# A row-wise log-sum-exp: row sums shared among group reductions, two-operand adds and ScalarE accumulation, and the last row loaded whole

## The chip, the cores and the metric

The kernel runs on one core of one Trainium2 chip. The metric is the device time in microseconds (us), lower is better. The profile's span, from the first to the last instruction, is some 1.8 us shorter than that time. Times inside a profile are counted from the start of its span.

## The reference

```python
x: float32 [32, 512, 1024], standard normal
def reference(x):
    max_x = np.max(x, axis=-1, keepdims=True)
    return max_x.squeeze(-1) + np.log(np.sum(np.exp(x - max_x), axis=-1))
```

That is 16384 rows of 1024 numbers, 128 rows on each of the 128 partitions: 67.1 MB are read and 64 KB written.

## The kernel before

It takes no maximum. It computes log(sum(exp(x))) directly, and if any sum left the range 1e-15 to 1e15 it runs a slow second pass with the maximum. Rows pass through a ring of 48 rows in SBUF. ScalarE makes the exponentials in place; then the row sums are made in one of three ways: "R", a VectorE reduction of up to 4 rows; "T", a VectorE instruction for each row that adds its two halves and accumulates; "A", ScalarE's own accumulation in the exponential.

```python
RING = 48
loads = [(16, "R")] * 5 + [(13, "T"), (10, "T"), (7, "T"), (5, "T"), (4, "T"), (3, "T"), (2, "T")]
loads += [(1, "A")] * 3
LAST = NC - 1                       # NC = 128 rows on each partition
SPLIT = 3 * d // 4
...
for size, how in loads:
    ...
    load(p0, c0, size)
    for b in range(0, size, 4):
        s = min(4, size - b)
        v = ring[:, p0 + b : p0 + b + s, :]
        if how == "A":
            exp_sum(v, c0 + b)
            continue
        nc.scalar.activation(out=v, in_=v, func=AF.Exp)
        if how == "R":
            nc.vector.reduce_sum(out=sumexp[:, c0 + b : c0 + b + s], in_=v, axis=AX.X)
            continue
        for r in range(b, b + s):
            lo = ring[:, p0 + r, 0:H]
            nc.vector.scalar_tensor_tensor(
                out=lo, in0=lo, scalar=1.0, in1=ring[:, p0 + r, H:d],
                op0=ALU.mult, op1=ALU.add, accum_out=sumexp[:, c0 + r : c0 + r + 1])
...
load(p0, LAST, 1, 0, SPLIT)         # the last row comes as 3/4 and 1/4
load(p0, LAST, 1, SPLIT, d)
exp_sum(ring[:, p0, 0:SPLIT], LAST)
nc.scalar.activation(out=res[:, EARLY:LAST], in_=sumexp[:, EARLY:LAST], func=AF.Ln)
check(0, LAST, 0)                   # clamp, compare, count by a matmul
exp_sum(ring[:, p0, SPLIT:d], NC)
nc.scalar.activation(out=res[:, LAST:NC], in_=sumexp[:, NC : NC + 1], func=AF.Ln, bias=sumexp[:, LAST:NC])
nc.sync.dma_start(out=out_view, in_=res)
for i, c in ((1, LAST), (2, NC)):   # clamp and compare each part of the last sum
    ...
    add_to_count(i, last=i == 2)
nc.vector.tensor_copy(out=nbad, in_=count)
outside = nc.values_load(nbad[0:1, 0:1], ...)        # read by all five engines
with tc.If(outside > 0, ...):       # the slow pass; not taken with this input
    ...
```

## Time and profile before

| | before |
|---|---|
| time, median of 4 runs | 166.50 us (166.48 to 166.58) |
| span of the profile | 164.6 us |
| DMA share of the span | 95.2% |
| busy: ScalarE, VectorE | 116.4, 116.0 us |

The first lines are from the page of the kernel before. The first has busy time, share of the span and number of instructions for each engine. "DMA" and "GB/s" have 40 equal slices of the span: the busy share of the DMA engines in tenths, and the rate. The last two are DMA queues, with packets, megabytes, and their share of the time of 16 engines.

```profile
...
PE 0.6 (0%) x6; PEld 0.3 (0%) x6; DVE 116.0 (70%) x117; ACT 116.4 (71%) x48; POOL 0.2 (0%) x4
...
DMA  7989998997998999899899899999998999999940
GB/s 255 494 366 414 510 398 366 510 478 319 478 510 366 398 510 414 350 510 478 350 446 510 366 398 414 440 466 406 428 458 388 439 420 423 422 419 421 403 170 18
...
q1 hardware_dynamic: 2592, 67.18, 95.2%
q14 instruction: 2, 0.02, 0.0%
...
```

ScalarE (ACT) and VectorE (DVE) are busy for 71 and 70% of the span; the DMA engines never rest until the second slice from the end. This is a load stream with compute behind it. Queue 14: 2 packets, 0.02 MB. It carries the engines' instructions: by the packet records one of the two comes at 132.7 us, inside the stream, the other at 163.8 us, after it.

The next lines are groups of instructions from the same page: line, engine, operation, out<-in, shape, count, then busy us and mean ns, then the engine's idle time before them and what ended it.

```profile
...
L100 ACT ACTIVATE ring<-ring 128x4096 f32<-128x4096 f32 (+3 forms) x34 | 110.1, 3304 | 44.4 <-DMA ring<-in_x_dram 44.2
L102 DVE TENSOR_REDUCE sumexp<-ring 128x4 f32<-128x4096 f32 x20 | 87.0, 4412 | 33.8 <-ACT ring L100 33.8
L106 DVE SCALAR_TENSOR_TENSOR ring<-ring 128x512 f32<-128x512 f32 x44 | 27.7, 688 | 8.8 <-ACT ring L100 8.7
L86 ACT ACTIVATE ring<-ring 128x1024 f32<-128x1024 f32 (+2 forms) x5 | 4.3, 869 | 0.0
...
```

Both engines' idle time is waiting for data or for each other; neither sets the pace until the end. The end is this part of the timeline of before (start us, duration us, engine, line, operation; PE is TensorE, SPq the queue that issues DMAs):

```profile
...
157.33 0.69 DVE L106 SCALAR_TENSOR_TENSOR ring<-ring 128x512 f32<-128x512 f32 x1
...
158.63 1.04 ACT L86 ACTIVATE ring<-ring 128x1024 f32<-128x1024 f32 x1
...
159.79 0.24 ACT L119 ACTIVATE res<-sumexp 128x47 f32<-128x47 f32 x1
159.79 0.23 DVE L70 TENSOR_SCALAR clamped<-sumexp 128x127 f32<-128x127 f32 x1 [1.77 <-ACT ring L86]
159.94 0.83 ACT L86 ACTIVATE ring<-ring 128x768 f32<-128x768 f32 x1
...
160.76 0.40 ACT L86 ACTIVATE ring<-ring 128x256 f32<-128x256 f32 x1
...
161.07 0.19 ACT L86 ACTIVATION_READ_ACCUMULATOR ring<-ring 128x1 f32 x1
...
161.29 0.29 ACT L122 ACTIVATE res<-sumexp 128x1 f32<-128x1 f32 x1
...
161.34 0.15 DVE L129 TENSOR_SCALAR bad<-sumexp 128x1 f32<-128x1 f32 x1
161.53 0.16 DVE L133 TENSOR_TENSOR bad<-bad,sumexp 128x1 f32<-128x1 f32 x1
161.61 0.35 SPq L125 DMA_DIRECT2D out_dram<-res  x1
...
161.75 0.19 PE L66 MATMUL count<-ones,bad 128*1 128x1 f32 x2 [0.26 <-DVE bad L133]
161.97 0.15 DVE L137 CAST nbad<-count 1x1 int32<-1x1 f32 x1 [0.28 <-PE count L66]
```

ScalarE is late: the 3/4 row landed at 159.28 us by the semaphore records of the trace and is begun at 159.94; the 1/4 row landed at 159.60 and is begun at 160.76. Its last sum is read out at 161.25. From there one path goes through Ln and the output DMA, the other through VectorE and TensorE to the cast at 161.97, whose value all engines must read before they may end. A long row of waits and branches closes the program, up to 164.61.

### The profile page before, as it was taken

The numbers are of one execution on the slowest core, as the hardware profiler recorded it, in microseconds if no ns is written. First come the engines' busy times: TensorE is split into PE (matmuls) and PEld (weight loads), VectorE is DVE, ScalarE is ACT, GpSimd is POOL, SyncE is SP. The second block draws the span as 40 slices with busy tenths as digits, with TensorE's granted clock in tenths as the row PEclk, the third lists the DMA queues.
The fourth block names the chain that finished last, engine by engine and source line by source line (L and its number), as shares of the span: only waits on it lengthen the run. The fifth ranks groups of instructions, "written<-read, shape, count | busy, mean of one in ns | idle before, by whom it ended". The sixth has DMA issues, their size and how long they took to land.

```text
span 164.6 us, 297 instructions
## 1 busy us (share of the span) xinstructions
PE 0.6 (0%) x6; PEld 0.3 (0%) x6; DVE 116.0 (70%) x117; ACT 116.4 (71%) x48; POOL 0.2 (0%) x4
## 2 busy tenths in 40 slices
PE   0000000000000000000000000000000000000001
PEld 0000000000000000000000000000000000000000
DVE  0000004999789995999959998699998668665951
ACT  3000039990699709994299915998799999999992
POOL 0000000000000000000000000000000000000000
DMA  7989998997998999899899899999998999999940
GB/s 255 494 366 414 510 398 366 510 478 319 478 510 366 398 510 414 350 510 478 350 446 510 366 398 414 440 466 406 428 458 388 439 420 423 422 419 421 403 170 18
DMA packets 2594, 67.19 MB, mean 408 GB/s; under 512 B 288, under 2 KB 544, under 8 KB 1056
## 3 DMA queue, kind: packets, MB, share of 16 engines
q1 hardware_dynamic: 2592, 67.18, 95.2%
q14 instruction: 2, 0.02, 0.0%
HBM read 67.11 MB, written 0.07 MB: 408 GB/s over the span
## 4 chain that ended last, share of the span: by engine, by line
DMA 66%; DVE 19%; ACT 12%; issue 1%; SPq 0%; PE 0%; ACTq 0%; DVEq 0%
DMA ring<-in_x_dram 66%; DVE sumexp L102 19%; ACT ring L100 9%; ACT ring L86 2%; SPq L81 0%; DVE bad L133 0%; DVE bad L129 0%; ACT res L119 0%; PE count L66 0%; DVE nbad L137 0%; ACTq L100 0%; DVEq L129 0%; ACTq L119 0%
## 5 line engine op out<-in xcount | busy, mean ns | idle before, releaser
L100 ACT ACTIVATE ring<-ring 128x4096 f32<-128x4096 f32 (+3 forms) x34 | 110.1, 3304 | 44.4 <-DMA ring<-in_x_dram 44.2
L102 DVE TENSOR_REDUCE sumexp<-ring 128x4 f32<-128x4096 f32 x20 | 87.0, 4412 | 33.8 <-ACT ring L100 33.8
L106 DVE SCALAR_TENSOR_TENSOR ring<-ring 128x512 f32<-128x512 f32 x44 | 27.7, 688 | 8.8 <-ACT ring L100 8.7
L86 ACT ACTIVATE ring<-ring 128x1024 f32<-128x1024 f32 (+2 forms) x5 | 4.3, 869 | 0.0
L106 DVE DVE_READ_ACCUMULATOR ring<-ring 128x1 f32 x44 | 3.7, 83 | 0.0
L62 ACT ACT_TABLE_LOAD x1 | 1.3, 1283 | 0.7 <-PEq L170 0.7
L70 DVE TENSOR_SCALAR clamped<-sumexp 128x127 f32<-128x127 f32 x1 | 0.2, 226 | 1.8 <-ACT ring L86 1.8
L66 PE MATMUL count<-ones,bad 128*1 128x1 f32 x6 | 0.6, 164 | 161.4 <-DVE clamped L74 160.4
L86 ACT ACTIVATION_READ_ACCUMULATOR ring<-ring 128x1 f32 x5 | 0.9, 186 | 0.0
L129 DVE TENSOR_SCALAR bad<-sumexp 128x1 f32<-128x1 f32 x2 | 0.3, 154 | 0.6 <-ACT ring L86 0.5
L63 DVE MEMSET ones<- 128x1 f32 x1 | 0.1, 59 | 0.8 <-PEq L170 0.8
L66 PEld LDWEIGHTS count<-ones,bad 128*1 128x1 f32 x6 | 0.3, 80 | 161.6 <-DVE clamped L74 160.4
L133 DVE TENSOR_TENSOR bad<-bad,sumexp 128x1 f32<-128x1 f32 x2 | 0.3, 160 | 0.1
L137 DVE CAST nbad<-count 1x1 int32<-1x1 f32 x1 | 0.1, 147 | 0.3 <-PE count L66 0.3
L74 DVE SCALAR_TENSOR_TENSOR clamped<-clamped,sumexp 128x127 f32<-128x127 f32 x1 | 0.3, 294 | 0.0
L122 ACT ACTIVATE res<-sumexp 128x1 f32<-128x1 f32 x1 | 0.3, 294 | 0.0
L119 ACT ACTIVATE res<-sumexp 128x47 f32<-128x47 f32 x1 | 0.2, 242 | 0.0
L114 ACT ACTIVATE res<-sumexp 128x80 f32<-128x80 f32 x1 | 0.3, 253 | 0.0
L170 POOL MEMSET const-bfloat16-1.0<- 128x1 bf16 x1 | 0.1, 102 | 0.0
L170 POOL MEMSET const-uint8-127<- 128x1 uint8 x1 | 0.1, 101 | 0.0
L170 POOL MEMSET const-float32-0.0<- 128x1 f32 x1 | 0.1, 99 | 0.2 <-issue 0.2
L170 POOL MEMSET const-float32-1.0<- 128x1 f32 x1 | 0.1, 98 | 0.0
(1 smaller groups left out, 0.1 us busy)
## 6 DMA issues: line engine op xcount, KB each, us to landing
ring<-in_x_dram SPq DMA_DIRECT2D x1, 6656.0 KB, 33.3
ring<-in_x_dram SPq DMA_DIRECT2D x1, 5120.0 KB, 30.4
ring<-in_x_dram SPq DMA_DIRECT2D x1, 3584.0 KB, 28.7
ring<-in_x_dram SPq DMA_DIRECT2D x1, 2560.0 KB, 30.4
ring<-in_x_dram SPq DMA_DIRECT2D x1, 2048.0 KB, 31.0
ring<-in_x_dram SPq DMA_DIRECT2D x1, 1536.0 KB, 30.4
ring<-in_x_dram SPq DMA_DIRECT2D x3, 512.0 KB, 33.3
ring<-in_x_dram SPq DMA_DIRECT2D x1, 1024.0 KB, 32.5
```

Of the source, the lines that this page charges most:

```text
L62: nc.scalar.preload_act_table_set("natural_log_exp_and_others")
L66: nc.tensor.matmul(count, lhsT=bad[:, i : i + 1], rhs=ones, start=i == 0, stop=last)
L74: nc.vector.scalar_tensor_tensor(out=clamped[:, c0:c1], in0=clamped[:, c0:c1], scalar=0.0, in1=sumexp[:, c0:c1], op0=ALU.bypass, op1=ALU.n ...
L86: nc.scalar.activation(out=v, in_=v, func=AF.Exp, accum_out=sumexp[:, c : c + 1])
L100: nc.scalar.activation(out=v, in_=v, func=AF.Exp)
L102: nc.vector.reduce_sum(out=sumexp[:, c0 + b : c0 + b + s], in_=v, axis=AX.X)
L106: nc.vector.scalar_tensor_tensor(out=lo, in0=lo, scalar=1.0, in1=ring[:, p0 + r, H:d], op0=ALU.mult, op1=ALU.add, accum_out=sumexp[:, c0 + ...
L114: nc.scalar.activation(out=res[:, 0:EARLY], in_=sumexp[:, 0:EARLY], func=AF.Ln)
L122: nc.scalar.activation(out=res[:, LAST:NC], in_=sumexp[:, NC : NC + 1], func=AF.Ln, bias=sumexp[:, LAST:NC])
L129: nc.vector.tensor_scalar(out=bad[:, 3:4], in0=sumexp[:, c : c + 1], scalar1=LOW, scalar2=HIGH, op0=ALU.max, op1=ALU.min,)
L133: nc.vector.tensor_tensor(out=bad[:, i : i + 1], in0=bad[:, 3:4], in1=sumexp[:, c : c + 1], op=ALU.not_equal)
L170: nc = _bacc.Bacc("TRN2", target_bir_lowering=False, num_devices=1)
```

## The change

Its intent: share the row sums so that both engines finish just behind the stream with fewer instructions, and shorten what follows the last byte. The last row comes whole. Its sum is checked in two ways that need little after it: from below, by the maximum of 256 raw values (if that is at least -34, the sum is above 1e-15); from above, by a matmul that adds the last sums straight into the count. The exponential of the last row goes to PSUM, so that the raw row stays. Three engines read the flag.

```diff
-    loads = [(16, "R")] * 5 + [(13, "T"), (10, "T"), (7, "T"), (5, "T"), (4, "T"), (3, "T"), (2, "T")]
-    loads += [(1, "A")] * 3
+    loads = [
+        "R8 R8", "R8 R8", "R8 R8", "R7 R6 A A", "R6 R5 A A A", "R5 R4 A", "R5 R4", "R5 T3",
+        "R3 A A A", "R3 A", "R2 T2", "R3", "R1 A", "T2", "T1", "A", "A",
+    ]
...
+    ENGINES = [mybir.EngineType.SP, mybir.EngineType.Activation, mybir.EngineType.DVE]
... (the loop over the loads, with declarations that spare waits which an earlier wait already covers)
+                o = v if c < LAST else last_exp
+                exp = nc.scalar.activation(out=o, in_=v, func=AF.Exp, accum_out=sums)
...
-    load(p0, LAST, 1, 0, SPLIT)
-    load(p0, LAST, 1, SPLIT, d)
... (the two sums of the split row and their two checks go)
+    nc.scalar.activation(out=res[:, EARLY:NC], in_=sumexp[:, EARLY:NC], func=AF.Ln)
     nc.sync.dma_start(out=out_view, in_=res)
... (clamp and compare of rows 0 to 126, as before)
+    nc.tensor.matmul(count, lhsT=bad[:, 0:1], rhs=far, start=True, stop=False)
+    nc.vector.reduce_max(out=bad[:, 2:3], in_=last_row[:, 0, 0 : d // 4], axis=AX.X)
+    nc.vector.tensor_scalar(out=bad[:, 1:2], in0=bad[:, 2:3], scalar1=LOG_LOW, scalar2=None, op0=ALU.is_lt)
+    nc.tensor.matmul(count, lhsT=bad[:, 1:2], rhs=far, start=False, stop=False)
+    nc.tensor.matmul(count, lhsT=sumexp[:, LAST:NC], rhs=ones, start=False, stop=True)
+    nc.vector.tensor_scalar(out=fine, in0=count, scalar1=HIGH, scalar2=None, op0=ALU.is_lt)
+    all_fine = nc.values_load(fine[0:1, 0:1], engines=ENGINES, ...)
+    with tc.If(all_fine < 1, ...):
```

More of the change, by code (lines that the diff above doesn't have):

```diff
@@ L10 @@
 LOW, HIGH = 1e-15, 1e15
+LOG_LOW = -34.0
 @with_exitstack
@@ L40 @@
     RING = 48
-    loads = [(16, "R")] * 5 + [(13, "T"), (10, "T"), (7, "T"), (5, "T"), (4, "T"), (3, "T"), (2, "T")]
-    loads += [(1, "A")] * 3
+    loads = [
+        "R8 R8", "R8 R8", "R8 R8", "R7 R6 A A", "R6 R5 A A A", "R5 R4 A", "R5 R4", "R5 T3",
+        "R3 A A A", "R3 A", "R2 T2", "R3", "R1 A", "T2", "T1", "A", "A",
+    ]
+    loads = [[(op[0], int(op[1:] or 1)) for op in load.split()] for load in loads]
+    assert sum(s for ops in loads for _, s in ops) == NC
+    ENGINES = [mybir.EngineType.SP, mybir.EngineType.Activation, mybir.EngineType.DVE]
+    EARLY = 104
     LAST = NC - 1
-    SPLIT = 3 * d // 4
-    EARLY = 80
-    assert sum(size for size, _ in loads) == LAST
     big = ctx.enter_context(tc.tile_pool(name="big", bufs=1))
@@ L52 @@
     ring = big.tile([P, RING, d], fp32, name="ring")
-    sumexp = stats.tile([P, NC + 1], fp32, name="sumexp")
+    sumexp = stats.tile([P, NC], fp32, name="sumexp")
     res = stats.tile([P, NC], fp32, name="res")
     clamped = stats.tile([P, NC], fp32, name="clamped")
-    bad = stats.tile([P, 4], fp32, name="bad")
+    bad = stats.tile([P, 3], fp32, name="bad")
+    fine = stats.tile([1, 1], i32, name="fine")
+    far = stats.tile([P, 1], fp32, name="far")
     ones = stats.tile([P, 1], fp32, name="ones")
-    nbad = stats.tile([1, 1], i32, name="nbad")
+    last_exp = psum.tile([P, 1, d], fp32, name="last_exp")
     count = psum.tile([1, 1], fp32, name="count")
@@ L63 @@
     nc.vector.memset(ones, 1.0)
-    def add_to_count(i, last=False):
-        nc.tensor.matmul(count, lhsT=bad[:, i : i + 1], rhs=ones, start=i == 0, stop=last)
-    def check(c0, c1, i):
-        nc.vector.tensor_scalar(
-            out=clamped[:, c0:c1], in0=sumexp[:, c0:c1],
-            scalar1=LOW, scalar2=HIGH, op0=ALU.max, op1=ALU.min,
-        )
-        nc.vector.scalar_tensor_tensor(
-            out=clamped[:, c0:c1], in0=clamped[:, c0:c1], scalar=0.0, in1=sumexp[:, c0:c1],
-            op0=ALU.bypass, op1=ALU.not_equal, accum_out=bad[:, i : i + 1],
-        )
-        add_to_count(i)
@@ L80, in load @@
-    def load(p0, c0, size, k0=0, k1=d):
-        nc.sync.dma_start(
-            out=ring[:, p0 : p0 + size, k0:k1], in_=x_rows[:, c0 : c0 + size, k0:k1]
-        )
-    def exp_sum(v, c):
-        nc.scalar.activation(out=v, in_=v, func=AF.Exp, accum_out=sumexp[:, c : c + 1])
-    c0 = 0
-    p0 = 0
-    for size, how in loads:
-        if p0 + size > RING:
-            p0 = 0
-        load(p0, c0, size)
-        for b in range(0, size, 4):
-            s = min(4, size - b)
-            v = ring[:, p0 + b : p0 + b + s, :]
-            if how == "A":
-                exp_sum(v, c0 + b)
-                continue
-            nc.scalar.activation(out=v, in_=v, func=AF.Exp)
-            if how == "R":
-                nc.vector.reduce_sum(out=sumexp[:, c0 + b : c0 + b + s], in_=v, axis=AX.X)
-                continue
-            for r in range(b, b + s):
-                lo = ring[:, p0 + r, 0:H]
-                nc.vector.scalar_tensor_tensor(
-                    out=lo, in0=lo, scalar=1.0, in1=ring[:, p0 + r, H:d],
-                    op0=ALU.mult, op1=ALU.add,
-                    accum_out=sumexp[:, c0 + r : c0 + r + 1],
-                )
-        c0 += size
-        p0 += size
-        if size == 10:
-            nc.scalar.activation(out=res[:, 0:EARLY], in_=sumexp[:, 0:EARLY], func=AF.Ln)
@@ L116 @@
-    load(p0, LAST, 1, 0, SPLIT)
-    load(p0, LAST, 1, SPLIT, d)
-    exp_sum(ring[:, p0, 0:SPLIT], LAST)
-    nc.scalar.activation(out=res[:, EARLY:LAST], in_=sumexp[:, EARLY:LAST], func=AF.Ln)
-    check(0, LAST, 0)
-    exp_sum(ring[:, p0, SPLIT:d], NC)
-    nc.scalar.activation(
-        out=res[:, LAST:NC], in_=sumexp[:, NC : NC + 1], func=AF.Ln, bias=sumexp[:, LAST:NC]
-    )
-    nc.sync.dma_start(out=out_view, in_=res)
-    for i, c in ((1, LAST), (2, NC)):
-        nc.vector.tensor_scalar(
-            out=bad[:, 3:4], in0=sumexp[:, c : c + 1],
-            scalar1=LOW, scalar2=HIGH, op0=ALU.max, op1=ALU.min,
-        )
-        nc.vector.tensor_tensor(
-            out=bad[:, i : i + 1], in0=bad[:, 3:4], in1=sumexp[:, c : c + 1], op=ALU.not_equal
-        )
-        add_to_count(i, last=i == 2)
@@ L137, with load, without_wait @@
-    nc.vector.tensor_copy(out=nbad, in_=count)
-    outside = nc.values_load(
-        nbad[0:1, 0:1], min_val=0, max_val=P * NC,
-        skip_runtime_bounds_check_because="a count of sums",
-    )
-    with tc.If(outside > 0, preferred_fallthrough_block=False):
+    nc.vector.memset(far, 100 * HIGH)
+    def load(p0, c0, size):
+        return nc.sync.dma_start(out=ring[:, p0 : p0 + size, :], in_=x_rows[:, c0 : c0 + size, :])
+    def without_wait(ins, group, reason):
+        tc.declare_no_dep(ins.ins, group=group, reason=reason)
@@ new lines @@
+    c = 0
+    p = 0
+    for ops in loads:
+        size = sum(s for _, s in ops)
+        if p + size > RING:
+            p = 0
+        dma = load(p, c, size).ins
+        for how, s in ops:
+            v = ring[:, p : p + s, :]
+            sums = sumexp[:, c : c + s]
+            if how == "A":
+                o = v if c < LAST else last_exp
+                exp = nc.scalar.activation(out=o, in_=v, func=AF.Exp, accum_out=sums)
+            else:
+                exp = nc.scalar.activation(out=v, in_=v, func=AF.Exp)
+            without_wait(exp, "loads", "the slot's earlier users came before this load")
+            without_wait(exp, "exps", "the slot's earlier users came before this load")
+            without_wait(exp, "sums", "the slot's earlier users came before this load")
+            tc.add_to_no_dep_group("exps", exp.ins)
+            added = []
+            if how == "R":
+                added = [nc.vector.reduce_sum(out=sums, in_=v, axis=AX.X)]
+            elif how == "T":
+                for r in range(s):
+                    lo = ring[:, p + r, 0:H]
+                    added.append(
+                        nc.vector.scalar_tensor_tensor(
+                            out=lo, in0=lo, scalar=1.0, in1=ring[:, p + r, H:d],
+                            op0=ALU.mult, op1=ALU.add, accum_out=sums[:, r : r + 1],
+                        )
+                    )
+            for add in added:
+                tc.declare_no_dep(add.ins, dma, reason="ScalarE has waited for it")
+                without_wait(add, "loads", "they came before this one")
+            for add in added:
+                tc.add_to_no_dep_group("sums", add.ins)
+            c += s
+            p += s
+            last_row = v
+        tc.add_to_no_dep_group("loads", dma)
+        if c == EARLY + 14:
+            nc.scalar.activation(out=res[:, 0:EARLY], in_=sumexp[:, 0:EARLY], func=AF.Ln)
@@ new lines @@
+    nc.scalar.activation(out=res[:, EARLY:NC], in_=sumexp[:, EARLY:NC], func=AF.Ln)
+    nc.sync.dma_start(out=out_view, in_=res)
+    nc.vector.tensor_scalar(
+        out=clamped[:, 0:LAST], in0=sumexp[:, 0:LAST],
+        scalar1=LOW, scalar2=HIGH, op0=ALU.max, op1=ALU.min,
+    )
+    nc.vector.scalar_tensor_tensor(
+        out=clamped[:, 0:LAST], in0=clamped[:, 0:LAST], scalar=0.0, in1=sumexp[:, 0:LAST],
+        op0=ALU.bypass, op1=ALU.not_equal, accum_out=bad[:, 0:1],
+    )
+    nc.tensor.matmul(count, lhsT=bad[:, 0:1], rhs=far, start=True, stop=False)
@@ new lines @@
+    nc.vector.reduce_max(out=bad[:, 2:3], in_=last_row[:, 0, 0 : d // 4], axis=AX.X)
+    nc.vector.tensor_scalar(
+        out=bad[:, 1:2], in0=bad[:, 2:3], scalar1=LOG_LOW, scalar2=None, op0=ALU.is_lt
+    )
+    nc.tensor.matmul(count, lhsT=bad[:, 1:2], rhs=far, start=False, stop=False)
+    nc.tensor.matmul(count, lhsT=sumexp[:, LAST:NC], rhs=ones, start=False, stop=True)
+    nc.vector.tensor_scalar(out=fine, in0=count, scalar1=HIGH, scalar2=None, op0=ALU.is_lt)
+    all_fine = nc.values_load(
+        fine[0:1, 0:1], engines=ENGINES, min_val=0, max_val=1,
+        skip_runtime_bounds_check_because="a truth value",
+    )
@@ L144 @@
+    with tc.If(all_fine < 1, preferred_fallthrough_block=False):
         for c0 in range(0, NC, RING):
@@ L152 @@
             nc.vector.reduce_sum(out=sumexp[:, c0 : c0 + s], in_=v, axis=AX.X)
-        nc.scalar.activation(out=res, in_=sumexp[:, 0:NC], func=AF.Ln)
+        nc.scalar.activation(out=res, in_=sumexp, func=AF.Ln)
         nc.vector.tensor_sub(out=res, in0=res, in1=clamped)
```

## The prediction

> **What bounds the kernel now.** The load stream. The page's DMA rows show the 16 DMA engines busy for 95.2% of the 164.6 us span. Full 16-row loads (8.39 MB) land every 19.35 us (semaphore records of the trace), which is 433 GB/s; the Trainium skill ("DMA: Bandwidth & Descriptors", Specifications) gives a ceiling of 435 GB/s; the trace agrees, so the stream has nothing left to give. ScalarE is busy 116.4 us and VectorE 116.0 us of 164.6 (busy table): slack on both.
>
> Fitting the durations of the packets by size (4 KB 161 ns, 64 KB 2418 ns) gives about 10 ns a packet plus the bytes, so one load costs about 0.09 us. Both kernels make 17 loads of the same bytes, so the stream should be equally long. It ends, on the slowest of the DMA engines, at 159.6 us. One engine is 0.47 us behind the 15 others from the 7-row load on; before that the gap is 0.07 us. The packet records show an 8 KB instruction fetch at 132.7 us just there.
>
> So only the tail, 159.6 to 164.6 us, can move. There (timeline) ScalarE is late: it starts the 3/4 row at 159.94 (landed 159.28), the 1/4 row at 160.76, and its last sum is out at 161.26. Then two paths run. Ln (0.29), output issue at 161.61, landing at 163.15. And the check: clamp, compare, matmul, compare, matmul, cast, ready at 162.12, then register loads (0.53), branches and closing semaphores, 2.45 us. The check path binds; the output lands some 0.24 us before it is needed.
>
> **What the change does.** Sums: about 107 rows by VectorE reduction (4412 ns per 4 rows), 8 by two-operand add (0.61 us each), 13 by ScalarE accumulation (1.04 us each). VectorE's total grows to about 121 us, ScalarE's stays near 114: off the critical path until the end. Groups of up to 8 rows start VectorE about 3.5 us later and free ring slots later, but laying the loads out with these durations each load is still issued more than 10 us before the stream needs it: no starving. Fewer instructions may push the instruction fetch out of the stream.
>
> Tail after: the last row lands whole at 159.2 (no fetch) to 159.6; ScalarE, nearly caught up, takes 1.13 us with its accumulator read: last sum at about 160.5 to 160.8 (before 161.26). Ln 0.24, output issued about 160.8 to 161.1: 0.5 to 0.8 us sooner. Check: clamp and compare of 127 sums, maximum of 256 raw values (estimate 0.33 us from the reduction's rate), comparison, matmuls and one compare from PSUM: ready about 161.3, against 162.12. VectorE's last adds end about 159.8, so this path may bind. Both give 0.7 to 0.8 us.
>
> **Prediction.** 165.7 us; 8 in 10 within 165.2 to 166.3. Faster by over 2%: 2%; within 2%: 97%; slower: 1%.
>
> **What would show it.** DMA share and GB/s as before, with no low slice before the last two; last landing 159.2 to 159.6; no wait of the DMA queue for VectorE that empties the stream; last ScalarE sum by 160.9; output issued near 161; the check's flag near 161.3; the same 2.4 us close after it.
>
> **What would make it wrong.** A ring slot freed too late, so the stream has a gap; VectorE over a microsecond late at the end, delaying the Ln; an instruction fetch in the last microseconds; a close that is shorter or longer because only three engines read the flag.

## The result, and the profile after

| | before | changed |
|---|---|---|
| time, median of 4 runs | 166.50 us | 165.47 us (165.18 to 165.87) |
| ratio | | 0.9939, interval 0.9917 to 0.9960 |
| span of the profile | 164.6 us | 164.1 us |
| DMA share | 95.2% | 95.7% |
| busy: ScalarE, VectorE | 116.4, 116.0 us | 116.8, 122.2 us |

A ratio is the mean time of one kernel's runs over that of the other's of the same rounds, so not quite the ratio of the medians. The profiled run of the changed kernel is the slowest of its four; the fastest had a span of 163.4 us.

The same lines of the page of the changed kernel:

```profile
...
PE 0.4 (0%) x6; PEld 0.2 (0%) x6; DVE 122.2 (74%) x44; ACT 116.8 (71%) x53; POOL 0.2 (0%) x4
...
DMA  7979998997997999899999989999999999999960
GB/s 256 511 335 431 511 399 367 511 463 304 511 431 335 511 450 404 374 464 479 433 447 419 433 365 449 419 432 440 417 439 415 433 425 419 415 421 423 409 248 20
...
q1 hardware_dynamic: 2592, 67.18, 95.7%
q14 instruction: 2, 0.02, 0.0%
...
```

```profile
...
L99 DVE TENSOR_REDUCE sumexp<-ring 128x8 f32<-128x8192 f32 (+7 forms) x20 | 116.2, 5854 | 38.2 <-ACT ring L92 38.2
L92 ACT ACTIVATE ring<-ring 128x8192 f32<-128x8192 f32 (+7 forms) x24 | 101.7, 4283 | 43.6 <-DMA ring<-in_x_dram 43.6
L90 ACT ACTIVATE ring<-ring 128x1024 f32<-128x1024 f32 x12 | 12.5, 1039 | 0.0
L104 DVE SCALAR_TENSOR_TENSOR ring<-ring 128x512 f32<-128x512 f32 x8 | 5.1, 684 | 0.0
...
```

ScalarE's work is nearly unchanged, VectorE's is 6 us more, with 44 instructions instead of 117. The stream looks the same. So does queue 14, but by the packet records both of its packets (163.5 and 163.8 us) now come after the stream. The end of the changed kernel, from its timeline:

```profile
...
158.70 1.04 ACT L90 ACTIVATE ring<-ring 128x1024 f32<-128x1024 f32 x1
...
159.38 0.69 DVE L104 SCALAR_TENSOR_TENSOR ring<-ring 128x512 f32<-128x512 f32 x1
...
159.74 1.00 ACT L90 ACTIVATE last_exp<-ring 128x1024 f32<-128x1024 f32 x1
...
160.19 0.23 DVE L127 TENSOR_SCALAR clamped<-sumexp 128x127 f32<-128x127 f32 x1
160.45 0.29 DVE L131 SCALAR_TENSOR_TENSOR clamped<-clamped,sumexp 128x127 f32<-128x127 f32 x1
...
160.66 0.41 DVE L136 TENSOR_REDUCE bad<-ring 128x1 f32<-128x256 f32 x1
160.69 0.18 ACT L90 ACTIVATION_READ_ACCUMULATOR last_exp<-ring 128x1 f32 x1
...
160.90 0.22 ACT L121 ACTIVATE res<-sumexp 128x24 f32<-128x24 f32 x1
161.11 0.15 DVE L137 TENSOR_SCALAR bad<-bad 128x1 f32<-128x1 f32 x1
161.15 0.35 SPq L122 DMA_DIRECT2D out_dram<-res  x1
...
161.32 0.19 PE L140 MATMUL count<-far,bad 128*1 128x1 f32 x2 [0.33 <-DVE bad L137]
...
161.37 0.19 PE L141 MATMUL count<-ones,sumexp 128*1 128x1 f32 x2
161.60 0.14 DVE L143 TENSOR_SCALAR fine<-count 1x1 int32<-1x1 f32 x1 [0.33 <-PE count L141]
```

The last row landed at 159.68 us in this run, and ScalarE began it 0.06 us later: it is no longer late. The last sum is read out at 160.87 (before: 161.25) and the flag is ready at 161.74 (before: 162.12). The reading of the flag now ends on VectorE's work and not on ScalarE's: VectorE makes its last add at 159.38 and runs without a rest through the clamp at 160.19, the compare and the maximum at 160.66 to the comparison at 161.11, for whose result TensorE waits (161.32).

### The profile page after: what moved, and what is told of

Its sections match the earlier page's. It is cut to its first block, busy times and chain, and to the rows that moved or that the text cites. A ratio compares the mean times of both kernels' runs of the same rounds, so it can differ in the third digit from the quotient of the medians.

```text
span 164.1 us, 205 instructions
## 1 busy us (share of the span) xinstructions
PE 0.4 (0%) x6; PEld 0.2 (0%) x6; DVE 122.2 (74%) x44; ACT 116.8 (71%) x53; POOL 0.2 (0%) x4
## 3 DMA queue, kind: packets, MB, share of 16 engines
q1 hardware_dynamic: 2592, 67.18, 95.7%
## 4 chain that ended last, share of the span: by engine, by line
DMA 64%; DVE 22%; ACT 11%; issue 1%; SPq 0%; PE 0%; DVEq 0%
DMA ring<-in_x_dram 64%; DVE sumexp L99 20%; ACT ring L92 11%; DVE ring L104 1%; SPq L72 0%; DVE bad L136 0%; DVE clamped L127 0%; PE count L140 0%; DVE bad L137 0%; DVE clamped L131 0%; DVE fine L143 0%; PE count L141 0%; DVEq L127 0%
## 5 line engine op out<-in xcount | busy, mean ns | idle before, releaser
L99 DVE TENSOR_REDUCE sumexp<-ring 128x8 f32<-128x8192 f32 (+7 forms) x20 | 116.2, 5854 | 38.2 <-ACT ring L92 38.2
L92 ACT ACTIVATE ring<-ring 128x8192 f32<-128x8192 f32 (+7 forms) x24 | 101.7, 4283 | 43.6 <-DMA ring<-in_x_dram 43.6
L90 ACT ACTIVATE ring<-ring 128x1024 f32<-128x1024 f32 x12 | 12.5, 1039 | 0.0
L104 DVE SCALAR_TENSOR_TENSOR ring<-ring 128x512 f32<-128x512 f32 x8 | 5.1, 684 | 0.0
L90 ACT ACTIVATION_READ_ACCUMULATOR ring<-ring 128x1 f32 x12 | 2.2, 186 | 0.0
L90 ACT ACTIVATE last_exp<-ring 128x1024 f32<-128x1024 f32 x1 | 1.0, 1005 | 0.0
L104 DVE DVE_READ_ACCUMULATOR ring<-ring 128x1 f32 x8 | 0.7, 82 | 0.0
L135 PE MATMUL count<-far,bad 128*1 128x1 f32 x2 | 0.2, 164 | 160.8 <-DVE clamped L131 160.8
L135 PEld LDWEIGHTS count<-far,bad 128*1 128x1 f32 x2 | 0.1, 80 | 160.8 <-DVE clamped L131 160.8
```

The source lines that it names most:

```text
L90: exp = nc.scalar.activation(out=o, in_=v, func=AF.Exp, accum_out=sums)
L92: exp = nc.scalar.activation(out=v, in_=v, func=AF.Exp)
L99: added = [nc.vector.reduce_sum(out=sums, in_=v, axis=AX.X)]
L104: nc.vector.scalar_tensor_tensor(out=lo, in0=lo, scalar=1.0, in1=ring[:, p + r, H:d], op0=ALU.mult, op1=ALU.add, accum_out=sums[:, r : r + 1],
L135: nc.tensor.matmul(count, lhsT=bad[:, 0:1], rhs=far, start=True, stop=False)
```

## The experiments

Two theories stood at the start. Theory A: the gain is made in the last 5 us, after the last landing; how rows 0 to 126 are summed doesn't matter. Rival B: the gain comes from fewer and larger instructions over the whole run.

For each run the records of the trace give four moments that the page does not print. The last column, the end less the last landing, is the tail. It proved steady: 4.41, 4.38 and 4.38 us in three profiles of the changed kernel, while the last landing itself moved by 0.6 us. "Behind" is how much later the slowest DMA engine finished the last load than the next slowest. The trace does not number the DMA engines; that it is one of them is read from the semaphore of a load, which counts sixteen completions, one for each engine, of which one comes late. A fetch is an 8 KB packet on the instruction queue inside the stream.

| run | ratio to before | fetch at us | behind | last landing | last sum | flag | output landed | end | tail |
|---|---|---|---|---|---|---|---|---|---|
| before | 1 | 132.7 | 0.47 | 159.60 | 161.25 | 162.12 | 163.15 | 164.61 | 5.01 |
| changed | 0.9939 | none | 0.32 | 159.68 | 160.87 | 161.74 | 162.70 | 164.09 | 4.41 |
| c0, changed again | 0.9937 | none | 0.01 | 159.41 | 160.58 | 161.45 | 162.41 | 163.79 | 4.38 |
| c1, changed again | 0.9928 | none | 0.03 | 159.05 | 160.22 | 161.09 | 162.05 | 163.44 | 4.38 |
| e1, old sums, new tail | 0.9966 | 131.8 | 0.52 | 159.69 | 160.88 | 161.43 | 162.74 | 163.93 | 4.24 |
| e2, new sums, old tail | 0.9994 | none | 0.11 | 159.28 | 161.13 | 161.99 | 163.03 | 164.48 | 5.20 |
| e8, e2 with adds at the end | 0.9985 | none | 0.07 | 159.06 | 160.64 | 161.50 | 162.54 | 164.00 | 4.94 |
| e3, flag read by five | 0.9945 | none | 0.12 | 159.32 | 160.49 | 161.35 | 162.32 | 163.77 | 4.45 |
| e4, changed with adds at the end | 0.9929 | none | 0.15 | 159.20 | 160.38 | 160.98 | 162.21 | 163.44 | 4.24 |
| e4b, the same | 0.9927 | none | 0.43 | 159.53 | 160.70 | 161.30 | 162.53 | 163.76 | 4.23 |
| e6, 40 idle memsets | 0.9963 | 138.4 | 0.39 | 159.59 | 160.76 | 161.63 | 162.58 | 163.98 | 4.39 |
| e7, 300 idle memsets | 1.0084 | 9.9, 27.7, 80.6 | 2.10 | 161.29 | 162.50 | 163.62 | 164.33 | 165.96 | 4.67 |
| e9, e4 with the sum checked | 0.9931 | none | 0.28 | 159.37 | 160.54 | 161.36 | 162.36 | 163.75 | 4.38 |

All kernels gave correct results. Runs of one set share the runs of before: c0, e1, e2 and e4; e3, e6, e7 and e8; c1, e4b and e9. Each set ran on another chip, so moments of different sets can differ by the chip as well. The intervals are about 0.0013 to either side in the first and third set and 0.0023 in the second, where before itself had one run at 167.27 us.

### c0 and c1: the changed kernel again

No edit.

> The changed kernel again, as the control of this set. Theory A (the gain is made in the last 5 us, after the stream has landed): 165.5 us, with single runs spread over some 0.7 us because its end waits for the last landing, which moves by a few tenths. Rival B (the gain comes from fewer and larger instructions over the whole run): 165.5 us as well, so this run only sets the level and the spread.

> The changed kernel once more, as the control beside the next two on one chip: ratio to the kernel before 0.9937, single runs over some 0.4 us.

Medians 165.37 and 165.22 us, against 166.37 and 166.56 of before: 0.9937 and 0.9928, as in the first measurement. The runs are spread over 0.4 us, as the last landing is. Part of that spread is explained by no record: in the first profile of the changed kernel, in e4b and in e9 one DMA engine is 0.30 to 0.45 us behind at the third load, with no fetch; in c0 and c1 none is.

### e1: the old sums with the new tail

```diff
-        "R8 R8", "R8 R8", "R8 R8", "R7 R6 A A", "R6 R5 A A A", "R5 R4 A", "R5 R4", "R5 T3",
-        "R3 A A A", "R3 A", "R2 T2", "R3", "R1 A", "T2", "T1", "A", "A",
+        "R4 R4 R4 R4", "R4 R4 R4 R4", "R4 R4 R4 R4", "R4 R4 R4 R4", "R4 R4 R4 R4",
+        "T4 T4 T4 T1", "T4 T4 T2", "T4 T3", "T4 T1", "T4", "T3", "T2", "A", "A", "A", "A",
```

(EARLY, the number of rows whose logarithm is taken early, is 80 again.)

> The changed kernel with the sizes of loads and the kinds of sums of the kernel before (20 reductions of 4 rows, 44 two-operand adds), but the last row whole and the new check. Theory A: the gain stays whole or grows: VectorE is done at about 158 us instead of 160.1, so the flag is ready at about 161.3 instead of 161.7; 165.2 to 165.5 us. Rival B: the gain is gone, 166.3 to 166.5 us.

165.75 us, 0.9966: between the two theories, and both expectations failed. The tail was even shorter than that of the changed kernel (4.24 us, since VectorE was done at 158.1 us), but the last row landed at 159.69. With it came an 8 KB instruction fetch at 131.8 us, after which one DMA engine stayed 0.53 us behind the others, against 0.20 before it. The same step stands in the kernel before (fetch at 132.7, from 0.07 to 0.48). Theory A had left that out: the new sums matter through the stream. This step of 0.33 us is not the whole of it: in the means of the times e1 is 0.42 us behind c0 of the same set (165.82 and 165.41 us) although its tail is 0.14 us shorter, so some 0.2 us of its later landing is not explained.

### e2 and e8: the new sums with the old tail

```diff
# e2, against the changed kernel
-        ... "T2", "T1", "A", "A",
+        ... "T2", "T1", "A",
+    load(p, LAST, 1, 0, SPLIT)
+    load(p, LAST, 1, SPLIT, d)
+    ... (from here to the branch as before: split sums, two checks, five readers)
# e8, against e2
-        "R2 T2", "R3", "R1 A",
+        "R2 T2", "T3", "T1 A",
```

> The sums and loads of the change for rows 0 to 126, but the split last row, the check of two partial sums and the flag read by five engines of the kernel before. Theory A: ScalarE has 3/4 of the row, the Ln and 1/4 of the row after about 159.65, last sum about 161.2, cast near 162.05, as before: 166.3 to 166.5 us. Rival B: the gain stays, 165.4 to 165.7 us.

> The sums of the change with the old tail (as in the run that gave 0.9994 of the kernel before), with the two last reductions made into 4 two-operand adds. There ScalarE sat idle for 0.34 us before the Ln, until VectorE had made the last add at 159.6 us. If that wait is why the new sums gained nothing under the old tail: it goes, the cast is ready near 161.6 us and 0.25 to 0.35 us are gained, ratio about 0.9975. If not: 0.9994.

e2 took 166.32 us, 0.9994: the whole gain is gone, as theory A said, though no fetch disturbed the stream and the last landing was 0.32 us earlier than before. Lines of e2's timeline show where that went; the bracket is the idle time before the instruction and what ended it:

```profile
...
158.90 0.69 DVE L121 SCALAR_TENSOR_TENSOR ring<-ring 128x512 f32<-128x512 f32 x1
...
159.69 0.22 ACT L141 ACTIVATE res<-sumexp 128x23 f32<-128x23 f32 x1 [0.34 <-DVE ring L121]
...
159.81 0.82 ACT L90 ACTIVATE ring<-ring 128x768 f32<-128x768 f32 x1
...
161.85 0.15 DVE L159 CAST nbad<-count 1x1 int32<-1x1 f32 x1 [0.28 <-PE count L70]
```

ScalarE sat idle for 0.34 us until VectorE had made its last add, because the Ln there comes ahead of the 3/4 row and needs that add. In e8 VectorE is done earlier, and its timeline has no such wait:

```profile
...
159.19 0.22 ACT L141 ACTIVATE res<-sumexp 128x23 f32<-128x23 f32 x1
...
159.32 0.83 ACT L90 ACTIVATE ring<-ring 128x768 f32<-128x768 f32 x1
...
161.36 0.14 DVE L159 CAST nbad<-count 1x1 int32<-1x1 f32 x1 [0.28 <-PE count L70]
```

Its tail is 0.26 us shorter than e2's (4.94 against 5.20), as expected. The time moved by less than its intervals can tell (0.9985): the six runs fall in two groups, 165.78 to 165.93 and 166.27 to 166.43, which I have not explained; the profile is of the fastest run.

### e3: the flag read by five engines

```diff
-        fine[0:1, 0:1], engines=ENGINES, min_val=0, max_val=1,
+        fine[0:1, 0:1], min_val=0, max_val=1,
```

> The changed kernel, with the flag read and the branch taken by all five engines again. In the profiles the time from the flag to the end is 2.34 us where three engines read it and VectorE's check ends last, 2.49 us in the kernel before and 2.48 in the run with the old tail. If the number of readers is the cause: the close goes back to about 2.49 us, ratio to the kernel before about 0.9945. If the cause is elsewhere (the output's landing, the order of the last waits): close 2.34 us, ratio 0.9937.

0.9945, not told apart from 0.9937. From the flag to the end it took 2.43 us, between the 2.35 of the changed kernel and the 2.49 of before. The trace's records of SyncE (SP), the engine that issues the DMAs, are not printed by the page; they show both steps. Against the changed kernel, SyncE has one semaphore wait more in the row that closes the program (8 instead of 7, 0.06 us), and 0.01 us each in its register load and at the very end: 0.08 us for the two more readers. Against before, the rest is SyncE's register load of the flag: 0.47 us in e3, 0.53 before. Why that load took longer there is open.

### e4 and e4b: two-operand adds in place of the last reductions

```diff
-        "R2 T2", "R3", "R1 A",
+        "R2 T2", "T3", "T1 A",
```

> The changed kernel with the 3-row and the 1-row reduction near the end replaced by 4 two-operand adds (about 2 us less VectorE work from 153 us on, 6 instructions more). Theory A, in which VectorE's end at 160.1 us holds the check: the clamp starts at about 159.9, the flag is ready at about 161.4 instead of 161.7, 0.15 to 0.3 us are gained: 165.2 to 165.35 us. Rival B: no gain or a small loss, 165.5 to 165.6 us.

> The kernel with 4 adds in place of the last two reductions, again, head to head with the changed kernel. If VectorE's end held the check: 0.1 to 0.25 us faster than the control of this set. If the first result (0.15 us, inside the intervals) was chance: equal to the control.

The tail was 4.24 and 4.23 us, 0.15 less than that of the changed kernel in all three of its profiles, so VectorE's end did hold the flag. From the timeline of e4b:

```profile
...
158.95 0.68 DVE L104 SCALAR_TENSOR_TENSOR ring<-ring 128x512 f32<-128x512 f32 x1
...
159.57 1.01 ACT L90 ACTIVATE last_exp<-ring 128x1024 f32<-128x1024 f32 x1
159.75 0.23 DVE L127 TENSOR_SCALAR clamped<-sumexp 128x127 f32<-128x127 f32 x1
...
160.22 0.41 DVE L136 TENSOR_REDUCE bad<-ring 128x1 f32<-128x256 f32 x1
...
160.98 0.35 SPq L122 DMA_DIRECT2D out_dram<-res  x1
161.16 0.14 DVE L143 TENSOR_SCALAR fine<-count 1x1 int32<-1x1 f32 x1 [0.33 <-PE count L141]
```

The last add starts at 158.95, the clamp follows ScalarE at 159.75, and the flag is ready 0.60 us after the last sum instead of 0.87. Only 0.15 of the 0.27 us shows. SyncE's records, c0 beside e4b, have the other 0.12 us. SyncE both issues the output DMA and reads the flag: it issues until 161.33, when the flag has been ready since 161.30, and its register load begins 0.09 us after the flag instead of 0.03; the load takes 0.48 us instead of 0.46; and its first closing wait passes at 162.55, just after the output's landing at 162.53 and 0.04 us later than in c0 after the branch before it. So the output path takes over, by its issue more than by its landing. In e1 the issue alone does it: there the register load begins 0.15 us after the flag. In the times it can't be resolved: 0.9929 beside 0.9937, then 0.9927 beside 0.9928. This is the best kernel by its tail, and a tie by its time.

### e6 and e7: instruction fetches put back

```diff
     nc.vector.memset(far, 100 * HIGH)
+    for _ in range(40):          # 300 in e7
+        nc.vector.memset(idle, 0.0)
```

> The changed kernel with 40 memsets of one scratch column on VectorE before its first sum, in time in which it waits for the first load. If the instruction fetch inside the stream is what the many small adds of the kernel before cost: an 8 KB fetch appears between 15 and 155 us, one DMA engine is some 0.3 us further behind from there on (last landing about 0.45 us after the 15th engine), and the time goes up by 0.2 to 0.35 us, ratio about 0.9955. If fetches don't matter: ratio 0.9937 and no such step.

> The same with 300 memsets (about 11 to 18 us of VectorE time, all before its first sum at 30 us). If fetches cost: two or three more fetches than without; where they fall to the same DMA engine the lag adds up to 0.6 to 1.0 us and the time goes to 166.0 to 166.4 us; where they fall to different engines the lag stays near 0.35 us and the time near 165.7. If fetches don't matter: ratio 0.9937.

These touch neither the tail nor the loads. In e6 a fetch came at 138.4 us, the slowest engine went from 0.10 to 0.40 us behind, the tail stayed at 4.39 us, and the time rose to 165.79 us, 0.9963 instead of the 0.9937 of c0: a little more than expected. The intervals of the two ratios overlap, and c0 is of another set. The nearest kernel of e6's own set is e3, with no fetch and a tail 0.06 us longer: its six runs are at 165.32 to 165.70 us and the five of e6 at 165.77 to 165.89, 0.28 us more in the mean. That agrees with the step of 0.3 us in the records. In e7 three fetches fell into the stream, and one DMA engine was behind by 0.31, then 1.23, then 2.17 us: the lags add up. The other fifteen engines ended the last load at 159.19 us, as in the other runs. The page shows two more packets on queue 14 (three in the stream and one after it, where the changed kernel has two after it):

```profile
...
q1 hardware_dynamic: 2592, 67.18, 94.6%
q14 instruction: 4, 0.03, 0.1%
...
```

The time was 167.80 us, more than the upper expectation of 166.4: the first of its fetches cost about 0.3 us, as those of before, e1 and e6 did (0.3 to 0.4), but after the second and third the engine was 0.9 and 1.0 us further behind. The page gives no reason for that, and no run here tests one. In e7, against the expectation, only 211 of the 300 memsets came before the first reduction and the others between the first reductions, so VectorE ran later than in the changed kernel; the last landing, 161.29 us against 159.05 to 159.68, is what carries the loss, and 0.3 us is the longer tail (4.67 us).

### e9: the last row's sum clamped and compared, not its raw values

```diff
# against e4
-    nc.vector.reduce_max(out=bad[:, 2:3], in_=last_row[:, 0, 0 : d // 4], axis=AX.X)
-    nc.vector.tensor_scalar(... scalar1=LOG_LOW, op0=ALU.is_lt)
+    nc.vector.tensor_scalar(out=bad[:, 2:3], in0=sumexp[:, LAST:NC], scalar1=LOW, scalar2=HIGH, op0=ALU.max, op1=ALU.min)
+    nc.vector.tensor_tensor(out=bad[:, 1:2], in0=bad[:, 2:3], in1=sumexp[:, LAST:NC], op=ALU.not_equal)
     nc.tensor.matmul(count, lhsT=bad[:, 1:2], rhs=far, ...)
-    nc.tensor.matmul(count, lhsT=sumexp[:, LAST:NC], rhs=ones, start=False, stop=True)
```

> The previous kernel with the last row's check on its sum (clamp and compare, two VectorE instructions and a matmul after the last sum, as before) in place of the maximum over raw values. From the durations of the kernel before: the flag is ready 0.86 us after ScalarE's last sum instead of 0.60; the output's landing hides about 0.1 us of it, so 0.1 to 0.2 us slower than the previous kernel. If the raw check is worth nothing: equal to it.

The flag was ready 0.82 us after the last sum instead of 0.60, and the tail was 4.38 us instead of 4.24: the raw check is worth 0.14 us where VectorE is done in time. In the changed kernel itself VectorE's late end spends it: there the flag comes 0.87 us after the last sum. The times (0.9931 and 0.9927) don't resolve it.

## Why the prediction was right or wrong

The time was inside the range: 165.47 us for a predicted 165.7, 0.2 us faster than the middle, and "within 2%" was right. The sum behind it was mis-sized in one term, and two smaller errors cancelled, which is luck: by the prediction's own moments the flag was due at 161.3 us and came at 161.43 in the mean of the three profiles of the changed kernel, while the close was put at 2.45 us and took 2.35.

- **The stream binds and only the end can move: right, but for one term.** Rate and loads stayed as they were. The step that was too small is "the stream has nothing left to give". It gave about 0.3 us: the profiles with one fetch have their last landing at 159.59 to 159.69 us, the nine with none at 159.05 to 159.68, 159.32 in the mean. That difference is all in the slowest engine: the other fifteen ended at 159.17 us in the mean with a fetch and at 159.16 without. The prediction saw the fetch, said that fewer instructions "may push the instruction fetch out of the stream", and put the last landing at "159.2 (no fetch) to 159.6"; it did not decide between the two. e6 shows what the fetch is worth: a step of 0.3 us in the records, and 0.28 us of time against e3 of its own set.
- **The tail: right in mechanism and nearly in size.** Predicted 0.7 to 0.8 us in all, some of it from an earlier landing; the tail itself went from 5.01 to 4.4 us, 0.6 us. ScalarE caught up, and the last sum came 1.17 to 1.19 us after the last landing (1.65 before). Predicted was the last sum at 160.5 to 160.8; the profiles have 160.22 to 160.87.
- **VectorE's end may bind: right.** Its last adds ended near 159.8 in the prediction, and at 160.08, 159.78 and 159.42 in the three profiles of the changed kernel, with their accumulator reads. e4 frees it and the tail falls by 0.15 us.
- **No starving: right.** The DMA row shows no low slice before the second from the end, and VectorE's 6 us of extra work cost nothing until the end.
- **"The same 2.4 us close": about right,** 2.35 in place of 2.49; of the 0.14 us, e3 gives 0.08 to the number of readers, and 0.06 is a shorter register load on SyncE.
- **The maximum over 256 values** took 0.415 us, not 0.33: the estimate came from the rate of long reductions and missed part of a fixed cost, by an estimate some 0.15 us (the sum of 1024 elements took 1.21 us, the maximum of 256 took 0.415).

Added up: 0.6 us of tail and 0.3 us of earlier landing are 0.9 us, against a measured 1.0 us. The profile shown above has the tail's part alone: it is the slowest run, and its last landing, 159.68 us, is no earlier than before's. That is how the two halves of the change hang together. The new tail alone gains 0.0034 (e1), the new sums alone 0.0006 (e2), both together 0.0061 to 0.0072. The sums take the fetch out of the stream but let VectorE end late; under the old tail its lateness eats the gain, under the new one it costs only 0.15 us.

What stays open: why after two of the fetches in e7 the engine fell back three times as far as after the others, some 0.2 us of e1's loss, what puts one engine behind at the third load in some executions without a fetch, and the two groups of times of e8. The declarations that spare waits stand in all the variants and were not tested alone.

## What to carry to other kernels

In a kernel bound by its loads, take the end apart against the last landing: end less last landing was steady to 0.03 us where whole times scattered by 0.4 to 0.7, and it resolved changes of 0.15 us that the times could not. Count the instructions of each engine too, even where no engine is busy: each instruction fetch that fell into the full load stream here left one DMA engine behind, by about 0.3 us or more, for the rest of the run. And when the work is shared out anew, look at which engine finishes last, not at their totals: two reductions too many at the end held the flag here.

## What the Trainium skill lacked or had wrong

- "Runtime: NRT & Kernel Launch", Instruction fetch mechanics, calls the cost of crossing a block "mostly hidden". For a full load stream beside it, it was not: a fetch put one DMA engine behind by 0.3 to 0.4 us in four cases and by 0.9 and 1.0 us in two, and the lags of three fetches added up to 2.1 us. The page gives blocks of 16 KiB; inside these streams each fetch was one packet of 8192 bytes.
- "DMA: Bandwidth & Descriptors", Queues, rings and completion order, says that each DMA engine goes round-robin between its queue rows and lists refill among the uses of row 14. The trace agrees with the sharing (a packet of queue 14, and then one engine's completion late for all later loads; the records do not number the engines), but the page has no measured cost of a refill; in the packet records each 8 KB fetch inside a stream took 0.31 to 0.33 us.
- No page gives a time for a program's own close after a flag: from the flag to the last instruction 2.34 to 2.50 us passed, of which 0.46 to 0.54 us were SyncE's register load.
